# All two-operand element-wise work moved from GpSimd to VectorE in a two-layer decoder step

## The chip, the core and the metric

The kernel runs on one core of a Trainium2 chip. The core has engines with an instruction queue each, worked off in order: TensorE (PE; PEld for its weight loads), VectorE (DVE), ScalarE (ACT), GpSimd (POOL) and SyncE (SP), which here only issues loads and stores. The metric is the device time of one execution in microseconds (us): less is better.

## What is computed

One inference step of a small decoder trunk for 512 prompt tokens and 8 sample tokens, model width 1024, all in float32. Layer A has multi-scale retention beside an attention into 256 memory tokens, layer B an attention to a window of 128 tokens with a sink per head, again beside memory attention. Each is followed by an MLP. Cut to what matters here:

```python
def rmsnorm(x, g):
    y = xf * lax.rsqrt(jnp.mean(xf * xf, axis=-1, keepdims=True) + EPS)
    return y * g

def sq_relu_mlp(x, g, w_up, w_down):          # w_up 1024 x 4096, w_down 4096 x 1024
    h = rmsnorm(x, g) @ w_up
    return jnp.square(jax.nn.relu(h)) @ w_down

def sink_softmax(s, sink):
    m = jnp.maximum(jnp.max(s, axis=-1, keepdims=True), sink)
    e = jnp.exp(s - m)
    return e / (jnp.sum(e, axis=-1, keepdims=True) + jnp.exp(sink - m))

# layer A: o = concat(silu(gate) * groupnorm(retention(q, k, v)), memory_attention)
# layer B: o = concat(window attention with ALiBi and sink_softmax, memory_attention)
# each:    x = x + o @ w_out;  x = x + sq_relu_mlp(x, ...);  at the end: rmsnorm(x, g_final)
```

## The kernel before

Activations lie feature by feature: eight tiles `x[kt]` of 128 partitions x 520 columns (512 prompt and 8 sample tokens), worked on in two halves of 256 and 264 columns. A product keeps nearly float32 precision by splitting each operand into a high part and a rest (both in the type fp32r) and summing three matmuls: high x high, high x rest, rest x high. So each operand, weight or activation, costs one copy on ACT (the high part) and one subtraction of two SBUF operands (the rest): L216 and L217 in `chunk` for weights, L179 and L180 in `Pair.put` for activations.

There are four stages: layer A (0 to about 283 us), the first MLP (265 to 650), layer B (620 to 850) and the second MLP (838 to the end at 1236). An MLP begins in `operands`, where VectorE scales the eight tiles (L278), makes the seven sums and differences of activations (L266) that a product by seven multiplications needs, splits them (L255) and adds up squares for the norm (L384). The first four up-projections of an MLP are direct products (L235), and their results wait for the chain of 1/sqrt (L397 to L365) and for L821. The others go in pairs through `seven`, 28 calls in all: L317 takes the rest of a weight combination, L322 (`total`) makes four sums or differences of weight blocks, 128x512, and L344 to L349 add up the products. Then come L829 (squared ReLU), L830 and the split (L179, L180). The down-projections (`d`) run beside the up-projections of the next group; L438 adds their results out of PSUM onto `x`.

In layer B the weights of the k/v and q projections (`kv0` to `kv3`, `qb0` to `qb7`) are first multiplied with the norm's gains (L214). `win_pair` does window attention for six heads and 128 queries at a time: scores `ws` (L503), copies with the bias out of PSUM (L690), maximum (L694), six exponentials on ACT (L700), the sums' reciprocal (L703), six multiplications by it (L705), transposes on TensorE (L713), copies of these on ACT (L715), products `wo`, and the split into `obh` and `obl`. The out-projection `ob` follows.

A framework of tiles sets the order: it schedules all instructions with a simulated timeline and writes them into the engines' queues. Strings such as ORDER_B only give the order in which the stages' pieces are handed to it. A changed engine or duration can thus change the order in other queues. Which engine does an element-wise step was chosen by tables: `engine()` reads a string with `p` for GpSimd and `v` for VectorE.

```python
ENG_R = dict(a='ppppvppv', m='pppppppv', f='vvvvvvvv', b='vvvvvpvv', y='vppppppv')   # L384
ENG_W = "pvppppvp"                                # L322: three of four on GpSimd
(nc.gpsimd if j % 3 in POOL_N else nc.vector)     # L705, POOL_N = (0, 1): four of six on GpSimd
```

## Time and profile before

| | |
|---|---|
| median of 3 runs | 1240.17 us (1239.22 to 1240.53) |
| the profiled execution | 1238.24 us, its span 1236.4 us |
| TensorE busy | 1196.2 us, 97% of the span |
| VectorE busy | 833.4 us, 67% |
| ACT busy | 534.6 us, 43% |
| GpSimd busy | 229.4 us, 19% |
| mean granted TensorE clock | 0.985 of full speed |

The busy shares are averages over stages with different limits; where TensorE stands idle, and for whom it waits, is read from the timeline of a stage. A timeline row gives the start and the time of an instruction (or of several alike, with their count behind the x), engine, line, operation, what it writes and reads, and in brackets how long the engine was idle before it and what ended that.

### The profile page before, as it was taken

What the parts mean: (1) busy time and instruction counts of PE and PEld (TensorE: products, weight loads), DVE (VectorE), ACT (ScalarE), POOL (GpSimd) and SP (SyncE); (2) the same over time, 40 slices, a digit from 0 to 9 for tenths busy, and PEclk for the clock granted to TensorE, in tenths of its full rate; (3) what the DMA queues carried; (4) which work ended last, traced back from release to release, by engine and by line L of the source; (5) the groups of instructions that cost most, each with busy time, mean ns of one, the idle gap of its engine ahead of it and who ended that gap; (6) DMA issues with size and microseconds to landing.
All of it is one profiled execution on the core that took longest, in us unless ns stands there. A gap on an engine that the chain in (4) does not pass through costs nothing. (4 is left out here: it accounts for less than half of the span.)

```text
span 1236.4 us, 23686 instructions
## 1 busy us (share of the span) xinstructions
PE 1196.2 (97%) x9718; PEld 1138.7 (92%) x9718; DVE 833.4 (67%) x1615; ACT 534.6 (43%) x999; POOL 229.4 (19%) x207
## 2 busy tenths in 40 slices
PE   8999999999999999999999998899799999999996
PEld 7999989999999999999999785579699999999996
DVE  7676777789766666675557558559796566666633
ACT  6232442355554444444324325455464444444532
POOL 2301100001312112121024114110222121121112
PEclk9999999999999999999999999899899999999998
DMA  8344622221223232232324354001132222323402
GB/s 304 112 151 168 217 77 72 88 86 71 73 97 120 86 116 91 97 106 75 121 99 143 107 163 141 30 1 68 36 103 103 82 107 86 120 86 104 140 32 69
DMA packets 43788, 128.25 MB, mean 104 GB/s; under 512 B 5112, under 2 KB 10368, under 8 KB 43552
## 3 DMA queue, kind: packets, MB, share of 16 engines
q1 hardware_dynamic: 41440, 119.80, 27.8%
q0 software_dynamic: 2240, 6.95, 1.5%
q8 instruction: 76, 1.25, 0.4%
q14 instruction: 32, 0.26, 0.1%
HBM read 117.65 MB, written 9.08 MB: 102 GB/s over the span
## 5 line engine op out<-in xcount | busy, mean ns | idle before, releaser
L438 DVE TENSOR_TENSOR xs<-d,xs 128x264 f32<-128x264 f32 (+1 forms) x128 | 54.0, 423 | 102.0 <-PE d L235 102.0
L235 PE MATMUL d<-hid,dw 128*128 128x256 f32 (+1 forms) x384 | 46.9, 283 | 0.0
L235 PEld LDWEIGHTS d<-hid,dw 128*128 128x128 f32 x384 | 46.3, 188 | 0.1
L830 ACT ACTIVATE u<-u 128x520 f32<-128x520 f32 x56 | 35.6, 636 | 21.5 <-DVE u L829 21.5
L639 POOL DMA_DIRECT2D out_ret_s<-s x12 | 6.9, 571 | 135.5 <-DVE s L638 102.8
L235 PE MATMUL ob<-obh,obw 128*128 128x256 f32 (+1 forms) x128 | 26.9, 297 | 2.4 <-ACT obh L179 1.6
L700 ACT ACTIVATE wp<-wp,wnm 128x256 f32<-128x256 f32 (+1 forms) x48 | 22.5, 469 | 12.6 <-DVE wes L697 8.6
L235 PEld LDWEIGHTS ob<-obh,obw 128*128 128x128 f32 x128 | 21.0, 193 | 5.0 <-ACT obh L179 3.0
L705 POOL TENSOR_SCALAR wp<-wp,wsm 128x256 f32<-128x256 f32 (+1 forms) x32 | 15.4, 498 | 54.8 <-ACT wp L700 28.5
L180 DVE TENSOR_TENSOR hid<-u,hid 128x520 fp32r<-128x520 f32 x32 | 23.3, 727 | 0.0
L829 DVE SCALAR_TENSOR_TENSOR u<-u,f0r 128x520 f32<-128x520 f32 x28 | 22.7, 811 | 0.4
L829 DVE SCALAR_TENSOR_TENSOR u<-u,f1r 128x520 f32<-128x520 f32 x28 | 22.7, 811 | 0.4
L524 ACT ACTIVATE p<-ms,nm 128x256 f32<-128x256 f32 x32 | 14.9, 476 | 18.5 <-DVE nm L522 16.8
L713 PEld LDWEIGHTS wt<-c,wp 128*128 128x128 f32 x84 | 9.8, 148 | 12.0 <-POOL wp L705 6.2
L179 ACT CAST hid<-u 128x520 fp32r<-128x520 f32 x32 | 20.1, 628 | 1.0
L713 PE MATMUL wt<-c,wp 128*128 128x128 f32 x84 | 15.7, 300 | 4.7 <-POOL wp L705 2.7
L235 PE MATMUL ob<-obl,obw 128*128 128x256 f32 (+1 forms) x64 | 18.1, 296 | 1.0 <-DVE obl L180 1.0
L522 DVE TENSOR_REDUCE nm<-ms 128x2 f32<-128x512 f32 x16 | 10.3, 685 | 11.8 <-PE ms L503 11.8
L180 DVE TENSOR_TENSOR obl<-wo,obh 128x128 fp32r<-128x128 f32 x24 | 6.9, 287 | 16.2 <-ACT obh L179 16.2
L503 PE MATMUL ws<-kvb,qb 64*128 64x256 f32 (+1 forms) x96 | 15.6, 407 | 1.2 <-DVE wp L690 0.6
L715 ACT COPY wpT<-wt 128x384 f32<-128x384 f32 x28 | 12.8, 479 | 8.2 <-PE wt L713 7.8
L690 DVE SCALAR_TENSOR_TENSOR wp<-cb,ws 128x256 f32<-128x256 f32 (+1 forms) x48 | 15.4, 375 | 0.1
(1997 smaller groups left out, 5124.6 us busy)
## 6 DMA issues: line engine op xcount, KB each, us to landing
kc<-in_mem_k SPq DMA_DIRECT2D x16, 256.0 KB, 4.1
vc<-in_mem_v SPq DMA_DIRECT2D x16, 256.0 KB, 4.4
s<-in_S SPq DMA_DIRECT2D x12, 256.0 KB, 4.9
out_ret_s<-s POOLq DMA_DIRECT2D x12, 256.0 KB, 2.5
xs<-in_xT SPq DMA_DIRECT2D x8, 260.0 KB, 4.3
memx<-in_memT SPq DMA_DIRECT2D x1, 1024.0 KB, 7.6
u004r<-in_w_up SPq DMA_DIRECT2D x2, 512.0 KB, 3.3
u006r<-in_w_up SPq DMA_DIRECT2D x2, 512.0 KB, 3.1
```

Of the source, the lines that this page charges most:

```text
L179: nc.scalar.copy(out=self.hi(kt, sl, rows), in_=src)
L180: eng.tensor_sub(out=self.lo(kt, sl, rows), in0=src, in1=f(self.hi(kt, sl, rows)))
L235: nc.tensor.matmul(t, w[:, ws], a(kt, HALVES[s]), start=kt == k[0] and m == 0, stop=kt == k[-1] and m == 2)
L438: nc.vector.tensor_add(out=x[mb][:, ts], in0=t, in1=x[mb][:, ts])
L503: i = m()
L524: nc.scalar.activation(out=t[:, b, :], in_=s[hh][:, b, :], func=AF.Exp, bias=nm[:, b:b + 1], accum_out=sm[:, b:b + 1])
L690: nc.vector.scalar_tensor_tensor(out=pv[:, j, :], in0=cb["nd"][:, k0:], scalar=float(SLOPES[6 * kb + j]), in1=sv[j // 3][j % 3], op0=ALU.m ...
L700: nc.scalar.activation(out=pv[:, j, :], in_=pv[:, j, :], func=AF.Exp, bias=nm[:, j:j + 1], accum_out=sm[:, j:j + 1])
L705: (nc.gpsimd if j % 3 in POOL_N else nc.vector).tensor_scalar(out=pv[:, j, :], in0=pv[:, j, :], scalar1=sm[:, j:j + 1], scalar2=1.0, op0=A ...
L713: nc.tensor.transpose(t[:, i * P:i * P + P], p[:, 3 * hh + i, kk * P:kk * P + P], ident)
L829: nc.vector.scalar_tensor_tensor(out=u[i], in0=u[i], scalar=0.0, in1=r[0], op0=ALU.max, op1=ALU.mult)
L830: nc.scalar.square(out=u[i], in_=u[i])
```

## The change

VectorE gets what GpSimd did on two operands: three of the four L322 in each call of `seven` (84 instructions), the additions of squares L384 (5 of `aacc`, 6 of `memacc`, 1 of `bacc`, 6 of `y0acc`), the six multiplications L606 in retention, the twelve L214, three L217 (`ob2`, `ob4`, `ob6`), one L180 in layer B and the last multiplications L1023 (8 of the first half, 3 of the second). Of the six multiplications L705 by the softmax's reciprocal, four now run on VectorE and two (j = 2 and 5) on ACT; before it was four on GpSimd and two on VectorE. GpSimd keeps the clearing of tiles and the issue of stores. The tables and `engine()` go, so that a line's number in the new file is about 10 lower (L322 is L312 there, L180 L170, L705 L698 and, for ACT, L696).

```diff
-ENG_R = dict(a='ppppvppv', m='pppppppv', f='vvvvvvvv', b='vvvvvpvv', y='vppppppv')
-ENG_W = "pvppppvp"
-POOL_W = (1, 4, 5)
-POOL_N = (0, 1)
+ACT_N = (2, 5)
...
-                    nc.gpsimd.tensor_tensor(out=w, in0=w, in1=gains[:, GAINS.index(by), :].unsqueeze(2).to_broadcast([P, KT, n // KT]),
+                    nc.vector.tensor_tensor(out=w, in0=w, in1=gains[:, GAINS.index(by), :].unsqueeze(2).to_broadcast([P, KT, n // KT]),
                                             op=ALU.mult)
                 nc.scalar.copy(out=wh[:, s], in_=raw[:, s])
-                eng.tensor_sub(out=wl[:, s], in0=raw[:, s], in1=f(wh[:, s]))
+                nc.vector.tensor_sub(out=wl[:, s], in0=raw[:, s], in1=f(wh[:, s]))
...
             def total(i, x0, x1, alu):
-                engine(ENG_W, i, turn).tensor_tensor(out=s[i], in0=x0, in1=x1, op=alu)
+                nc.vector.tensor_tensor(out=s[i], in0=x0, in1=x1, op=alu)
...
-                    engine(ENG_R[self.name[0]], 0 if self.direct else kt).tensor_add(out=acc, in0=acc, in1=sq)
+                    nc.vector.tensor_add(out=acc, in0=acc, in1=sq)
...
-            nc.gpsimd.tensor_mul(out=qw, in0=q[:, P:T].rearrange("p (n q) -> p n q", q=P),
+            nc.vector.tensor_mul(out=qw, in0=q[:, P:T].rearrange("p (n q) -> p n q", q=P),
...
-                    (nc.gpsimd if j % 3 in POOL_N else nc.vector).tensor_scalar(
-                        out=pv[:, j, :], in0=pv[:, j, :], scalar1=sm[:, j:j + 1], scalar2=1.0, op0=ALU.mult, op1=ALU.mult)
+                    if j in ACT_N:
+                        nc.scalar.mul(out=pv[:, j, :], in_=pv[:, j, :], mul=sm[:, j:j + 1])
+                    else:
+                        nc.vector.tensor_scalar(out=pv[:, j, :], in0=pv[:, j, :], scalar1=sm[:, j:j + 1], scalar2=None, op0=ALU.mult)
...
-                (nc.vector if s and kt not in TAIL_P else nc.gpsimd).tensor_mul(out=y, in0=y, in1=r)
+                nc.vector.tensor_mul(out=y, in0=y, in1=r)
```

VectorE at the start of the second MLP, where the last tiles of `operands` are split and the first call of `seven` (its sums are `u104s`) begins; before:

```order
L255 TENSOR_TENSOR f_10147<-f1t_10183,f_10147 128x260
L266 TENSOR_TENSOR f1t_10213<-f1t_10209,f1xg_10189 128x260
L255 TENSOR_TENSOR f_10122<-f1t_10198,f_10122 128x260
L255 TENSOR_TENSOR f_10134<-f1t_10209,f_10134 128x260
L322 TENSOR_TENSOR u104s_10556<-u104s_10556,u104r_10549 128x512
L180 TENSOR_TENSOR hid_10110<-f1xg_10238,hid_10110 128x520
L255 TENSOR_TENSOR f_10142<-f1xg_10238,f_10142 128x260
```

The same place after:

```order
L312 TENSOR_TENSOR u104s_10556<-u104r_10550 128x512
L374 TENSOR_TENSOR f1acc<-f1acc,f1sq_10229 128x520
L312 TENSOR_TENSOR u104s_10557<-u104r_10549,u104r_10550 128x512
L245 TENSOR_TENSOR f_10147<-f1t_10183,f_10147 128x260
L256 TENSOR_TENSOR f1t_10213<-f1t_10209,f1xg_10189 128x260
L245 TENSOR_TENSOR f_10122<-f1t_10198,f_10122 128x260
L245 TENSOR_TENSOR f_10134<-f1t_10209,f_10134 128x260
L170 TENSOR_TENSOR hid_10110<-f1xg_10238,hid_10110 128x520
L245 TENSOR_TENSOR f_10142<-f1xg_10238,f_10142 128x260
L245 TENSOR_TENSOR f_10150<-f1xg_10238,f_10150 128x260
L312 TENSOR_TENSOR u104s_10556<-u104s_10556,u104r_10549 128x512
```

Two sums of weights now stand ahead of the split L180 of the last tile (L170 after), and the one that stood there before follows it.

ACT in the first block of window attention, where `wp_9080` and `wp_9141` are the score tiles of two groups of six heads and queries, `wpT` the copies of transposes; before:

```order
L700 ACTIVATE wp_9080,wsm<-wp_9080,wnm 128x256 x4
L698 ACTIVATE wes<-wes 128x6
L700 ACTIVATE wp_9141,wsm<-wp_9141,wnm 128x256 x6
L715 COPY wpT_9114<-wt_9110 128x384
L715 COPY wpT_9120<-wt_9116 128x384
L753 ACTIVATE wses<-wsnm,sinks 128x1
L754 ACTIVATE wsp_9338,wssm<-wsp_9338,wsnm 128x129
L715 COPY wpT_9175<-wt_9171 128x384
```

After:

```order
L690 ACTIVATE wp_9080,wsm<-wp_9080,wnm 128x256 x2
L696 ACTIVATE wp_9039<-wp_9039,wsm 128x128 x2
L690 ACTIVATE wp_9080,wsm<-wp_9080,wnm 128x256 x2
L688 ACTIVATE wes<-wes 128x6
L169 CAST obh_8827<-wo_8894 128x128
L690 ACTIVATE wp_9141,wsm<-wp_9141,wnm 128x256
L707 COPY wpT_9114<-wt_9110 128x384
L690 ACTIVATE wp_9141,wsm<-wp_9141,wnm 128x256 x2
L707 COPY wpT_9120<-wt_9116 128x384
L690 ACTIVATE wp_9141,wsm<-wp_9141,wnm 128x256 x3
L696 ACTIVATE wp_9080<-wp_9080,wsm 128x256 x2
L169 CAST obh_8827<-wo_9028 128x128
```

The two multiplications of `wp_9080` (L696) stand behind the last exponential of `wp_9141`; the two of `wp_9141` and then the copy `wpT_9175` follow.

TensorE in the second block, where `wt_9627` and `wt_9633` are the transposes of the softmax tile `wp_9597`; before:

```order
L503 MATMUL ws_9763<-kvb,qb_7822 128x256
L503 MATMUL ws_9761<-kvb,qb_7822 128x256
L713 MATMUL wt_9627<-c,wp_9597 128x128 x3
L235 MATMUL ob_9840<-obh_8155,ob3h 128x256
L235 MATMUL ob_9840<-obl_8157,ob3h 128x256
```

After:

```order
L493 MATMUL ws_9763<-kvb,qb_7822 128x256
L493 MATMUL ws_9761<-kvb,qb_7822 128x256
L225 MATMUL ob_9840<-obh_8155,ob3h 128x256
L225 MATMUL ob_9840<-obl_8157,ob3h 128x256
L225 MATMUL ob_9840<-obh_8155,ob3l 128x256
```

Before the transposes, 14 matmuls of the out-projection `ob` are now in the queue (three of them shown), which stood behind them.

## Rows read from the trace of the kernel before

**Rows 1.** The page's first part: busy us (share) and instructions of each engine.
```profile
PE 1196.2 (97%) x9718; PEld 1138.7 (92%) x9718; DVE 833.4 (67%) x1615; ACT 534.6 (43%) x999; POOL 229.4 (19%) x207
```

**Rows 2.** Table by stretch: us, busy of PE, PEld, DVE, ACT, POOL; PEclk, DMA, GB/s.
```profile
310.00:341.00 31.00, 29.42 (x245) 29.01 (x243) 24.24 (x32) 16.65 (x29) 10.49 (x6) 1.00 0.22 74
...
740.00:770.00 30.00, 25.39 (x191) 17.80 (x189) 25.69 (x57) 16.12 (x44) 11.70 (x10) 1.00 0.38 125
770.00:800.00 30.00, 24.50 (x156) 16.49 (x156) 15.94 (x73) 15.77 (x61) 6.22 (x14) 0.93 0.16 53
800.00:830.00 30.00, 26.92 (x167) 21.00 (x164) 18.75 (x62) 16.03 (x60) 5.82 (x12) 0.84 0.00 1
860.00:890.00 30.00, 21.65 (x141) 20.10 (x140) 25.72 (x61) 12.10 (x26) 7.48 (x3) 0.83 0.18 64
...
1060.00:1160.00 100.00, 100.00 (x834) 99.91 (x833) 64.49 (x82) 44.33 (x67) 18.81 (x14) 1.00 0.26 91
```

**Rows 3.** Timeline of POOL and DVE in the second MLP, two calls of `seven`.
```profile
1080.83 1.29 POOL L322 TENSOR_TENSOR u130s<-u130r 128x512 f32<-128x512 f32 x1 [19.05 <-DMA u130r<-in_w_up]
1082.08 1.30 POOL L322 TENSOR_TENSOR u130s<-u130r,u130r 128x512 f32<-128x512 f32 x1
...
1082.16 1.77 DVE L322 TENSOR_TENSOR u130s<-u130s,u130r 128x512 f32<-128x512 f32 x1 [2.20 <-POOL u130s L322]
...
1106.80 0.68 DVE L322 TENSOR_TENSOR u132s<-u132r,u132s 128x512 f32<-128x512 f32 x1
1107.40 0.42 DVE L438 TENSOR_TENSOR xs<-d,xs 128x264 f32<-128x264 f32 x1
```

**Rows 4.** Timeline of DVE and PE at the start of the first MLP.
```profile
303.09 1.75 DVE L322 TENSOR_TENSOR u004s<-u004s,u004r 128x512 f32<-128x512 f32 x1 [1.18 <-POOL u004s L322]
...
305.29 1.06 DVE L401 SCALAR_TENSOR_TENSOR rv<-rz,rv 104x5 f32<-104x5 f32 x1
...
312.33 0.50 PE L235 MATMUL u<-hid,u002h 128*128 128x256 f32 x2 [0.98 <-DVE u L821]
```

**Rows 5.** Timeline of POOL, DVE and PE at the start of the second MLP.
```profile
866.68 4.59 POOL L322 TENSOR_TENSOR u104s<-u104r 128x512 f32<-128x512 f32 x1 [40.66 <-ACT f L254]
...
871.30 1.74 DVE L322 TENSOR_TENSOR u104s<-u104s,u104r 128x512 f32<-128x512 f32 x1 [1.16 <-POOL u104s L322]
...
873.58 1.85 DVE L255 TENSOR_TENSOR f<-f1xg,f 128x260 fp32r<-128x260 f32 x2
...
873.71 0.38 PE L235 MATMUL u<-hid,u100h 128*128 128x256 f32 x1 [4.10 <-DVE hid L180]
...
915.11 0.39 PE L300 MATMUL u110a<-f,u110l 128*128 128x260 f32 x1 [0.88 <-DVE u110l L317]
```

**Rows 6.** Timeline in window attention; last row, PE's waits: us, times, longest.
```profile
757.36 1.78 DVE L217 TENSOR_TENSOR obw<-ob1r,obw 128x1024 fp32r<-128x1024 f32 x1
759.67 1.21 DVE L217 TENSOR_TENSOR obw<-ob5r,obw 128x1024 fp32r<-128x1024 f32 x1
765.50 1.90 DVE L740 COPY kwc<-kvb 128x2 f32<-128x2 f32 x2
...
773.19 0.49 ACT L700 ACTIVATE wp<-wp,wnm 128x256 f32<-128x256 f32 x1
...
777.33 0.52 PE L713 MATMUL wt<-c,wp 128*128 128x128 f32 x3 [0.89 <-ACT wpT L715]
...
811.51 1.93 POOL L705 TENSOR_SCALAR wp<-wp,wsm 128x256 f32<-128x256 f32 x4 [25.87 <-ACT wp L700]
...
811.35 0.84 DVE L705 TENSOR_SCALAR wp<-wp,wsm 128x256 f32<-128x256 f32 x2
...
815.15 0.33 PE L713 MATMUL wt<-c,wp 128*128 128x128 f32 x1 [1.88 <-POOL wp L705]
...
PE wt L713 <- POOL wp L705: 2.7, 5, 1.9
```

**Rows 7.** Timeline of DVE at the end: the last multiplications.
```profile
1228.81 3.44 DVE L1023 TENSOR_TENSOR xs<-xs,y1r 128x264 f32<-128x264 f32 x5 [1.22 <-ACT y1r L411]
```

More of the change, by code (lines that the diff above doesn't have):

```diff
@@ L46 @@
 ORDER_F = "uddudduddudd"
-ENG_UL = "vvvvvvvv"
-ENG_R = dict(a='ppppvppv', m='pppppppv', f='vvvvvvvv', b='vvvvvpvv', y='vppppppv')
-ENG_B = "pvvvvvvv"
-ENG_W = "pvppppvp"
 BUFS_W = dict(wr=3, wh=3, wl=3)
@@ L56 @@
 BUFS_B = dict(blk=2, wp=3, mp=4, wpT=6, ld=5)
-TAIL_P = (3, 5, 7)
 STORES = ((1, 3, 5, 7), (0, 2, 4, 7))
 KEEP = 4
-POOL_W = (1, 4, 5)
-POOL_N = (0, 1)
+ACT_N = (2, 5)
 ORDER_B = "kasakkskasqqsaqwqwqwwqWwWWwWooSSSoSowWWowoWWoo"
@@ L148, in ld @@
             return blk(name, shape, "ld")
-        def engine(choice, i, turn=0):
-            return nc.gpsimd if choice[len(choice) // 2 * (turn % 2) + i] == "p" else nc.vector
         def small(name, shape, tag=None):
@@ L176, in lo, with put @@
                 return self._at("l", kt)[rows, sl]
-            def put(self, kt, src, sl=slice(0, TT), rows=slice(0, P), eng=nc.vector):
+            def put(self, kt, src, sl=slice(0, TT), rows=slice(0, P)):
                 nc.scalar.copy(out=self.hi(kt, sl, rows), in_=src)
-                eng.tensor_sub(out=self.lo(kt, sl, rows), in0=src, in1=f(self.hi(kt, sl, rows)))
+                nc.vector.tensor_sub(out=self.lo(kt, sl, rows), in0=src, in1=f(self.hi(kt, sl, rows)))
         gains = cp.tile([P, len(GAINS), KT], F32, name="gains")
@@ L202, in gain, with chunk @@
             return gains[:, GAINS.index(name), kt:kt + 1]
-        def chunk(src, n, name, place=None, eng=nc.vector, by=None):
+        def chunk(src, n, name, place=None, by=None):
             raw = wp.tile([P, n], F32, name=f"{name}r", tag="wr", bufs=BUFS_W["wr"])
@@ L249, in split, with cut @@
                 out=a.lo(kt), in0=x[kt], scalar=gain(g, kt), in1=f(a.hi(kt)), op0=ALU.mult, op1=ALU.subtract)
-        def cut(op, j, src, eng):
+        def cut(op, j, src):
             h, l = op[:, 0, j, :], op[:, 1, j, :]
             nc.scalar.copy(out=h, in_=src)
-            eng.tensor_sub(out=l, in0=src, in1=f(h))
+            nc.vector.tensor_sub(out=l, in0=src, in1=f(h))
         def operands(name, g, scale, direct, norm):
@@ L272, in put @@
                     op[i] = half(f"{name}{i}", F32R, [P, 2, UK, EVEN])
-                cut(op[i], j, src, nc.vector)
+                cut(op[i], j, src)
             for n, kt in enumerate(BY_PAIR):
@@ L301, in times, with seven @@
                                      stop=j == nj - 1 and m == 2, skip_group_check=more)
-        def seven(src, op, u, name, turn):
+        def seven(src, op, u, name):
             n = UK * P
@@ L316, in parts @@
                 nc.scalar.copy(out=h[:, c], in_=t)
-                engine(ENG_UL, (1, 5, 3, 4).index(ids[0]), turn).tensor_sub(out=l[:, c], in0=t, in1=f(h[:, c]))
+                nc.vector.tensor_sub(out=l[:, c], in0=t, in1=f(h[:, c]))
                 for i, k in enumerate(ids):
@@ L826, in up @@
                     u = [blk(f"u{l}{g}{n}{i}", tag="u") for i in range(2)]
-                    seven([d["w_up"][l, g * FK + n + i] for i in range(2)], op, u, f"u{l}{g}{n}", n // 2)
+                    seven([d["w_up"][l, g * FK + n + i] for i in range(2)], op, u, f"u{l}{g}{n}")
                     for i in range(2):
@@ L953, in layer_b @@
             for kt in range(KT):
-                b.put(kt, x[kt], eng=engine(ENG_B, kt))
+                b.put(kt, x[kt])
             m = rms("b", "wp")
@@ L1003, in project_out @@
                     t = half(f"obw{n}", F32R, [P, 2, KT * P]) if n < KEEP else None
-                    ahead.append(weights(*src(mb), t if t is None else [t[:, 0], t[:, 1]], nc.gpsimd if n in POOL_W else nc.vector))
+                    ahead.append(weights(*src(mb), t if t is None else [t[:, 0], t[:, 1]]))
                 t = part(f"ob{mb}", s)
```

## The prediction

> **What bounds the kernel now.** I read four views, in this order. The page's first part says who is busy: TensorE 1196.2 of 1236.4 us, VectorE two thirds, GpSimd a fifth [rows 1]. So at most 40.2 us can be had, and only where TensorE stands idle. The table by stretch says where that is [rows 2]. In the steady stretch of the MLP (1060 to 1160) TensorE is busy for all 100 us while VectorE has 35 us free; what is won or lost on VectorE there moves nothing. TensorE is idle for 1.58 us at the start of the first MLP, 4.61, 5.50 and 3.08 in window attention, 8.35 at the start of the second MLP: 23.1 of the 40.2 in five short stretches. In two of them, 740 to 770 and 860 to 890, VectorE is busy for 25.7 us of 30. There VectorE sets the time, and an instruction more or less on it shows.
>
> Third, the timeline of VectorE beside that of GpSimd. In the MLP VectorE's L322, 128x512 with two operands in SBUF, takes 0.68 us at 1106.80, where GpSimd is idle, and 1.77 at 1082.16, where GpSimd began a L322 of its own at 1082.08 [rows 3]. So the engines get in each other's way there, at some 1.1 us a time. GpSimd suffers too: its first `u104s` takes 4.59 us beside a VectorE that is never idle [rows 5], against 1.29 at 1080.83, beside one that waits. Fourth, TensorE's waits, in the stretches named: they end on VectorE, or on GpSimd's softmax operation L705 [rows 4 to 6].
>
> **What VectorE gets, and whether it can carry it.** 84 of L322 at 0.68 [rows 3] are 57.1 us; 12 of L214 and 3 of L217 at 1.21 [rows 6] 18.2; six 128x520 additions of L384 and one L180 at the same price 4.8; 23 operations of 128x256 or 264 (12 of L384, 11 of L1023) at 0.42, the price of an L438 [rows 3], 9.7; six of L606 (128x384) at about 0.55, an estimate between the two sizes, 3.3; 16 more of L705 at 0.42, half of 0.84 [rows 6], 6.7. In all 100 us, so 833 become at most 933, 75% of the span, less what the stretching gives back. ACT gets 16 of L705 at about 0.49, the price of the nearest row, L700 [rows 6]: 8 us. Over the whole, nobody becomes the bound; what counts are the five stretches.
>
> **The steady MLP: nothing.** Per call of `seven` VectorE gets three L322 and loses one or two stretches of 1.1; the next instruction starts 0.60 us after an L322 [rows 3], so that is 1.8 against 1.1 to 2.2. It has a third of its time free, and TensorE is full. Without that cover some 24 steady calls at up to 0.7 us would cost 17 us; the 35 us of free time in 100 speak against it. A wait is added: the first L322 of a call now stands in VectorE's own queue until its weights have landed, with L829 and the L438 that empty TensorE's banks behind it. GpSimd stood so at 1080.83; but VectorE was idle then anyway and waited on, for GpSimd, to 1082.16 [rows 3]. I take 0. Layer B's L214 lies between 638 and 740, where TensorE has matmuls of the last down-projections and of other weights to do; there too I take 0.
>
> **Start of the first MLP: -2.0 us.** VectorE waits 1.18 us for GpSimd's L322 at 303.09, and its own takes 1.75 instead of 0.68 [rows 4]: 2.25 lost. In exchange it gets three L322 at 0.6, 1.8. That looks even, but the chain of 1/sqrt behind it has an instruction on 104x5 elements (L401) of 1.06 [rows 4], stretched like the others, an estimated 0.9. The chain ends 2.25 + 0.9 - 1.8 = 1.3 sooner, and TensorE's wait of 0.98 on L821 behind it goes. A wait for VectorE's L317 like the one of 0.88 at 915.11 [rows 5] stands at 341 too and, following GpSimd's L322, goes as well: 1.0. Bounds: 0, if the three L322 push as much as the stretches return, and -2.2.
>
> **Start of the second MLP: -2.5 us.** The same place, with VectorE full from 838 to 884. There 1.16 (wait) + 1.06 (L322, 1.74) + 1.0 (two L255 of 128x260 in 1.85, against two of 0.42) are lost [rows 5]. The new order puts two L322 ahead of the L180 for which TensorE waits 4.10 us at 873.71, in place of one with its wait (VectorE's queue, before and after, under The change). That L180 comes 1.16 + 1.06 + 0.6 - 2 x 0.6 = 1.6 sooner. At the end of VectorE's chain, where L821 begins, the sum is 3.2 - 3 x 0.6 = 1.4 sooner. To this comes TensorE's wait of 0.88 for `u110l` at 915.11 [rows 5]. Bounds: +1.8 (nothing returns, three L322 more) and -3.2 - 0.9 = -4.1. I take -1.6 - 0.9 = -2.5, since the stretches stand in these very rows.
>
> Here a rule speaks against the change. The Trainium skill, Perfetto Trace Analysis, section Optimizing Scalar/DVE Operations, says that where VectorE is saturated, giving work to ScalarE or even GpSimd may make sense, and adds that between VectorE and GpSimd it might not help since they share a read port. By its first half this place would get 1.8 us slower, by its second half and the rows it gets faster: the trace sides with the second half (1.74 us beside GpSimd against 0.68 alone).
>
> **Window attention, first block (750 to 787): +1.7 us.** Three L217 (ob2, ob4, ob6) enter VectorE's full stretch: 3 x 1.2 = 3.6. It gets back 0.57 of one L217 (1.78 against 1.21 [rows 6]) and about 2 us in tiny operations beside GpSimd (two copies of 128x2 take 1.90 [rows 6]); +1.0 is left. On ACT the order does harm: the two multiplications of a block stand behind the six exponentials of the *next* one (ACT's queue there). GpSimd normalised beside ACT; now the transposes wait for an ACT that is already without a gap (L700 at 0.49, row upon row [rows 6]) and for whose copies TensorE already waits 0.89 at 777.33. Four multiplications of 0.4 and two of 0.33 are an estimated 2.3 us (less than L700, which also sums). Some of it is covered, since VectorE does its four in 1.2 us where GpSimd took 1.93. Bounds: 0 and +4; I take +1.7.
>
> **Window attention, second block (806 to 836): -2.2 us.** TensorE waits 1.88 us at 815.15 for GpSimd, whose four L705 take 1.93 beside VectorE's two in 0.84 [rows 6]. The new order pulls 14 matmuls of `ob` ahead of these transposes (TensorE's queue there), of which 834 run in the 100 us of the steady stretch [rows 2], 0.12 each: 1.7 us of work in this gap, and ACT is free then. All five waits of this kind make 2.7 us [rows 6]; I take 1.7 and 0.5 of the other 0.8. Bounds: -2.7, and 0 if ACT's multiplications come later than GpSimd's did.
>
> **Start and tail: -0.5 us.** In the first 22 us VectorE gets five L384 at 0.6 and loses their stretching of its own instructions: even, 0. At the end its five L1023 took 3.44 us beside GpSimd's three [rows 7]; eight at 0.36, an estimate from the 0.42 less overlap, are 2.9: -0.5. Bounds: -1.5 and +0.5.
>
> Sum: -2.0 - 2.5 + 1.7 - 2.2 - 0.5 = -5.5. The profiled execution took 1238.24 us, so 1232.7; the median of the runs, 1240.17, stands 1.9 above it, so 1234.6.
>
> **Rivals.**
> *Slower, through ACT and VectorE in window attention.* Mechanism: normalisation on ACT behind the next block's exponentials, and three L217 ahead of VectorE's copies out of PSUM. At its bounds the first block costs +4, the second brings nothing; the `ob` work pulled ahead is then missing later, when the exponentials of the third block run, up to +1.9. With start and tail at 0 and the two MLP starts at -1.0 each, the sum is 4 + 1.9 - 2.0 = +3.9: 1244. It decides as soon as ACT's L705 ends later than TensorE has other matmuls to do. For it: ACT's rows without a gap from 770 to 778. Against it: only 16 of 30 us busy there on the whole [rows 2]. 0.18.
> *No difference.* The MLP starts bring -2.5 together, window attention costs +2: 1239 to 1240. For it: TensorE at 97%, and gains at a start that wait next on ACT's copy before L821. 0.18.
> *More.* TensorE's granted clock is 0.83 and 0.84 on the mean of 860 to 890 and 800 to 830 [rows 2]: full clock with pieces at 1.2 instead of 2.4 GHz, which follow idle times. If the idle times go, so may these pieces: 16% of 30 us, some 5 us in each, of which VectorE's chain hides the greater part. With half of it, -5 more: 1229.6. 0.12.
> *The change doesn't do what it says.* The scheduler also reorders the matmuls; the loss could be at any place. It is contained in the first rival's price. 0.02, at 1244.
> My forecast (1231 to 1237): 0.50.
>
> **Numbers.** A measurement tells 0.2% of this kernel, 2.5 us, from no change. Faster: the forecast and the "more" case, 0.62; the same 0.18; slower 0.20. The range of 8 in 10 reaches from 1228 to 1243: below it a third of "more", above it half and more of the slower ones.
>
> **What would show it.** Right: no two-input instruction of VectorE above 1.3 us at 128x512; `u104s` without a wait ahead of it and TensorE's 4.10 at 873 near 2.5; the 1.88 at 815 gone; the rows of 1.85 and 1.75 near 0.8 and 0.7. Wrong: TensorE waiting for ACT in 774 to 786 by more than 2 us above before (the first rival), or TensorE in the MLP below 99%, which would mean that VectorE's queue holds up its copies out of PSUM while an L322 waits for its weights.

## The result: 0.7% slower

The changed kernel takes 1248.45 us (median of 4 runs, 1247.97 to 1250.27), the kernel before 1239.88 beside it. The ratio is 1.0068, with a 95% interval of 1.0055 to 1.0082: some 8.4 us slower, where 5.5 us faster was predicted and 1243 was the upper end of the range. The profiled execution took 1247.97 us, its span is 1246.2, against 1238.24 and 1236.4 before.

The page's first part for the kernel after, busy time and instructions of each engine, which answers to [rows 1]:

```profile
PE 1200.8 (96%) x9718; PEld 1141.4 (92%) x9718; DVE 849.2 (68%) x1766; ACT 538.9 (43%) x1015; POOL 21.4 (2%) x40
```

Two things are to be seen. VectorE took over 100 us of work by the prediction's estimate, and is busy only 15.8 us longer: the stretching did go, and was larger than I thought. And the span grew by 9.8 us. TensorE stands idle for 5.2 of them (45.4 against 40.2) and is busy for 4.6 more with the same 9718 matmuls. Some 2.6 of the 4.6 are its lower clock (mean granted clock 0.983 against 0.985), at places shown below; the other 2.0, of which 1.1 in layer A, where the order of the matmuls changed, can't be put to single rows.

The table by stretch of the kernel after, in the columns of [rows 2] (us, busy of PE, PEld, DVE, ACT, POOL, then PEclk); the last four rows are stretches of [rows 2], the first three are at places that the prediction did not look at:

```profile
250.00:260.00 10.00, 8.00 (x59) 7.35 (x58) 6.94 (x22) 3.04 (x5) 0.00 (x0) 0.94 0.01 2
259.00:262.00 3.00, 3.00 (x15) 3.00 (x15) 3.00 (x6) 2.02 (x5) 0.00 (x0) 0.50 0.07 12
650.00:690.00 40.00, 35.23 (x272) 33.43 (x271) 28.02 (x55) 14.59 (x30) 1.67 (x3) 0.96 0.37 124
...
740.00:770.00 30.00, 27.71 (x201) 21.90 (x201) 19.87 (x59) 15.85 (x46) 2.96 (x4) 1.00 0.27 83
770.00:800.00 30.00, 22.32 (x138) 14.74 (x137) 19.10 (x61) 20.20 (x70) 2.01 (x3) 0.83 0.48 153
860.00:890.00 30.00, 24.98 (x197) 24.27 (x195) 30.00 (x63) 18.23 (x38) 0.00 (x0) 0.95 0.20 72
1060.00:1160.00 100.00, 100.00 (x836) 100.00 (x835) 68.47 (x100) 44.15 (x66) 0.00 (x0) 1.00 0.29 101
```

Two of these places stood in the trace of before as full ones:

```profile
250.00:260.00 10.00, 9.96 (x84) 9.76 (x83) 6.09 (x12) 4.07 (x7) 0.00 (x0) 1.00 0.14 55
650.00:690.00 40.00, 39.74 (x326) 37.00 (x324) 29.87 (x61) 17.71 (x40) 15.35 (x11) 1.00 0.40 135
```

So TensorE lost 2.0 us in 10 at the end of layer A, and 4.5 us in 40 where layer B's projections begin. Of the stretches that the prediction did look at, 740 to 770 and 860 to 890 are fuller than before (27.71 and 24.98 against 25.39 and 21.65), 770 to 800 is emptier (22.32 against 24.50). Such stretches compare roughly only, since the stages lie up to 14 us later by then. To say what each stage contributed, I compared in the two timelines the start of TensorE's first matmul with the same weight tile, and took the differences from one such mark to the next. The last two columns say how much of a difference is idle time of TensorE, and how much is lower clock (half of the time in which it was busy at a granted clock of 0.5); what is left over is neither.

| place | predicted, us | measured, us | of it idle | of it clock |
|---|---|---|---|---|
| start, to the first `qkv00h` | 0 | -2.6 | -1.6 | -1.7 |
| layer A, to `oa1h` at 260 | not priced | +5.3 | +2.5 | +1.7 |
| start of the first MLP, to `u010l` | -2.0 | +1.5 | +0.1 | +1.7 |
| steady first MLP, to 589 | 0 | -0.2 | 0 | 0 |
| layer B, projections (L214), to `qb3h` | 0 | +6.5 | +4.5 | +1.6 |
| window attention, first block, to `ob2h` | +1.7 | +2.8 | +1.1 | +1.4 |
| window attention, second block, to `ob7h` | -2.2 | +0.7 | +0.9 | -0.4 |
| start of the second MLP, to `u110l` | -2.5 | -2.9 | -1.2 | -1.7 |
| steady second MLP | 0 | -0.2 | 0 | 0 |
| tail, to the end | -0.5 | -1.1 | -1.1 | 0 |

The two positive entries that decide, 5.3 and 6.5, are at places to which the prediction gave nothing. The idle column is what an engine's queue can explain. The clock column is less certain to come again: of each kernel one execution was profiled, and the mean granted clock of the four executions of the kernel after lies between 0.978 and 0.983.

### The profile page after: what moved, and what is told of

Its sections match the earlier page's. It is cut to its first block, busy times and chain, and to the rows that moved or that the text cites. A ratio compares the mean times of both kernels' runs of the same rounds, so it can differ in the third digit from the quotient of the medians.

```text
span 1246.2 us, 23531 instructions
## 1 busy us (share of the span) xinstructions
PE 1200.8 (96%) x9718; PEld 1141.4 (92%) x9718; DVE 849.2 (68%) x1766; ACT 538.9 (43%) x1015; POOL 21.4 (2%) x40
## 4 chain that ended last, share of the span: by engine, by line
PE 55%; issue 34%; DVE 7%; ACT 2%; DMA 1%; SPq 0%; DVEq 0%; POOL 0%; POOLq 0%; ACTq 0%
PE d L225 15%; PE qkv L225 9%; PE qb L225 3%; PE ga L225 3%; PE kv L225 1%; PE ob L225 1%; ACT wp L690 1%; PE ms L493 1%; PE memv L478 1%; PE memk L467 1%; DVE wp L680 1%; DVE f L245 1%; PE u L225 1%; PE mt L526 1%; PE mo L493 1%
## 5 line engine op out<-in xcount | busy, mean ns | idle before, releaser
L428 DVE TENSOR_TENSOR xs<-d,xs 128x264 f32<-128x264 f32 (+1 forms) x128 | 54.0, 424 | 107.1 <-PE d L225 107.1
L170 DVE TENSOR_TENSOR hid<-u,hid 128x520 fp32r<-128x520 f32 x32 | 22.1, 692 | 0.0
L705 PEld LDWEIGHTS wt<-c,wp 128*128 128x128 f32 x84 | 10.4, 154 | 12.4 <-ACT wpT L707 6.2
L705 PE MATMUL wt<-c,wp 128*128 128x128 f32 x84 | 16.7, 318 | 4.8 <-ACT wpT L707 4.2
L821 DVE SCALAR_TENSOR_TENSOR u<-u,f0r 128x520 f32<-128x520 f32 x28 | 19.5, 696 | 0.4
L821 DVE SCALAR_TENSOR_TENSOR u<-u,f1r 128x520 f32<-128x520 f32 x28 | 19.5, 696 | 0.4
L170 DVE TENSOR_TENSOR obl<-wo,obh 128x128 fp32r<-128x128 f32 x24 | 6.9, 287 | 15.5 <-ACT obh L169 15.4
L627 DVE TENSOR_TENSOR kvs<-rb,ks 128x512 f32<-128x512 f32 x12 | 8.2, 686 | 9.6 <-PE rb L625 9.6
L493 PEld LDWEIGHTS ws<-kvb,qb 64*128 64x128 f32 x96 | 9.9, 197 | 5.2 <-DVE wp L680 3.0
```

The source lines that it names most:

```text
L170: nc.vector.tensor_sub(out=self.lo(kt, sl, rows), in0=src, in1=f(self.hi(kt, sl, rows)))
L428: nc.vector.tensor_add(out=x[mb][:, ts], in0=t, in1=x[mb][:, ts])
L493: i = m()
L705: nc.tensor.transpose(t[:, i * P:i * P + P], p[:, 3 * hh + i, kk * P:kk * P + P], ident)
L821: nc.vector.scalar_tensor_tensor(out=u[i], in0=u[i], scalar=0.0, in1=r[0], op0=ALU.max, op1=ALU.mult)
```

## The experiments

### One part at a time

Six kernels are the kernel before with one part of the change. The ratios compare with executions of the kernel before made beside each run (medians 1239.47 to 1240.34), and the microseconds behind a ratio are worked out from it. All twelve L214 on VectorE:

```diff
-                    nc.gpsimd.tensor_tensor(out=w, in0=w, in1=gains[:, GAINS.index(by), :]...
+                    nc.vector.tensor_tensor(out=w, in0=w, in1=gains[:, GAINS.index(by), :]...
```

> The kernel before, with nothing changed but the twelve L214 (weights times gains) moved from GpSimd to VectorE. Theory A: an L214 stands at the head of VectorE's queue until its weights have landed, and what empties TensorE's banks and the 1/sqrt chain wait behind it: +5 to +7 us against the kernel before (about 1245 to 1247), VectorE idle on DMA for some 10 us between 635 and 690, and TensorE behind by 5 to 7 us from the k/v projection on. Theory B: it is only the added work, 12 x 1.2 us on a VectorE with free time: 0 to +2 us, no idle time of VectorE on DMA ahead of the 1/sqrt chain.

Measured: 1242.39 us, ratio 1.0022 (1.0005 to 1.0039), +2.7 us.

The softmax's normalisation as after: four of six on VectorE, two on ACT.

```diff
-                    (nc.gpsimd if j % 3 in POOL_N else nc.vector).tensor_scalar(
...
+                    if j in ACT_N:
+                        nc.scalar.mul(out=pv[:, j, :], in_=pv[:, j, :], mul=sm[:, j:j + 1])
+                    else:
+                        nc.vector.tensor_scalar(out=pv[:, j, :], in0=pv[:, j, :], scalar1=sm[:, j:j + 1], scalar2=None, op0=ALU.mult)
```

> The kernel before, with only the softmax multiplication L705 as in the changed kernel: four of six on VectorE, two on ACT. Theory A: the two on ACT stand behind the next block's exponentials and hold the transposes up: +2 to +4 us (1242 to 1244), with TensorE's waits for ACT's copies of transposes up by 2 us. Theory B: the loss in window attention comes from the three L217 in VectorE's full stretch, and L705 alone gives -2 to 0 us, since GpSimd's 1.93 us go.

Measured: 1242.89 us, ratio 1.0028 (1.0012 to 1.0044), +3.5 us.

The six multiplications L606 of retention on VectorE:

```diff
-            nc.gpsimd.tensor_mul(out=qw, in0=q[:, P:T]...
+            nc.vector.tensor_mul(out=qw, in0=q[:, P:T]...
```

> The kernel before, with only the six L606 of retention moved to VectorE. Theory A: it is L606 that changes the order of TensorE's matmuls in layer A, so that other work runs out before the last head of retention is done: +3 to +5 us (1243 to 1245), TensorE idle for about 2 us between 240 and 262. Theory B: the order changes through the additions of squares L384 at the start; L606 alone gives -0.5 to +0.5 us.

Measured: 1241.90 us, ratio 1.0031 (1.0019 to 1.0044), +3.9 us, for six instructions of half a microsecond. The ten executions reach from 1239.87 to 1245.41, and the difference of the medians is 2.4 only; the profiled one is the slowest of them.

All sums of weights L322 on VectorE:

```diff
-ENG_W = "pvppppvp"
+ENG_W = "vvvvvvvv"
```

> The kernel before, with only L322 (all four sums of a call) on VectorE. Theory A: stretching and waiting at the start of the second MLP go, nothing else changes: -2 to -4 us (1236 to 1238), TensorE's wait for the split L180 at 873 from 4.1 to about 2.5 us, steady MLP at 100%. Theory B: the gain seen there in the changed kernel came with its other order of things, or is lost again at the start of the first MLP: -0.5 to +1 us.

Measured: 1238.30 us, ratio 0.9991 (0.9981 to 1.0001), -1.1 us: no difference that can be told.

The three L217 on VectorE:

```diff
-POOL_W = (1, 4, 5)
+POOL_W = ()
```

> The kernel before, with only the three L217 of ob2, ob4 and ob6 moved to VectorE. Theory A: they stand in VectorE's full stretch of window attention, but their own stretching of other instructions goes: 0 to +1.5 us. Theory B: they hold up the copies out of PSUM by their whole 3.6 us: +2 to +4 us.

Measured: 1241.43 us, ratio 1.0009 (1.0000 to 1.0018), +1.1 us.

Start and tail: the additions of squares L384 (one of them in layer B), layer B's one L180 and the last multiplications L1023:

```diff
-ENG_R = dict(a='ppppvppv', m='pppppppv', f='vvvvvvvv', b='vvvvvpvv', y='vppppppv')
-ENG_B = "pvvvvvvv"
+ENG_R = dict(a='vvvvvvvv', m='vvvvvvvv', f='vvvvvvvv', b='vvvvvvvv', y='vvvvvvvv')
+ENG_B = "vvvvvvvv"
...
-                (nc.vector if s and kt not in TAIL_P else nc.gpsimd).tensor_mul(out=y, in0=y, in1=r)
+                nc.vector.tensor_mul(out=y, in0=y, in1=r)
```

> The kernel before, with the sums of squares L384, the L180 and the last multiplications L1023 on VectorE; L322, L214, L217, L606 and L705 stay where they were. Theory A: the 2.4 us that the changed kernel gained in its first 22 us and the 1.1 us at its end come from these: -2.5 to -4 us (1235.5 to 1237). Theory B: the gain at the start came with the other order in retention (L606): -1 to 0 us.

Measured: 1235.97 us, ratio 0.9967 (0.9956 to 0.9979), -4.1 us.

What follows: the six sum up to +6.0 us, the whole change costs +8.4. The difference of 2.4 lies within the intervals taken together (about 4), so the parts nearly add up. Three parts cost, L214, L606 and the softmax; one gains, the ends; L322, with 84 instructions the largest part by far, makes no difference that can be told. The softmax, L606 and L217 fell into the range of their first theory, the ends just beyond it; L214 and L322 fell between their two theories, so their times decide nothing.

### Layer B: work or waiting?

Why L214 costs is read from VectorE's timeline in the kernel after. The rows that matter from 655 to 676:

```profile
655.26 1.23 DVE L204 TENSOR_TENSOR kv2r<-kv2r,gains 128x1024 f32<-128x1024 f32 x1 [2.77 <-DMA kv2r<-in_w_kv]
...
668.04 0.69 DVE L374 TENSOR_TENSOR bacc<-bacc,bsq 128x520 f32<-128x520 f32 x1
668.75 1.23 DVE L204 TENSOR_TENSOR qb0r<-qb0r,gains 128x1024 f32<-128x1024 f32 x1
671.42 1.23 DVE L204 TENSOR_TENSOR qb1r<-qb1r,gains 128x1024 f32<-128x1024 f32 x1 [1.45 <-DMA qb1r<-in_w_in_b]
...
673.70 0.16 DVE L387 TENSOR_SCALAR rv<-bms 104x5 f32<-104x5 f32 x1
...
675.91 0.17 DVE L355 SCALAR_TENSOR_TENSOR ry<-rqt,rqu 104x5 f32<-104x5 f32 x1
```

The multiplications (L204 now) stand ahead of the norm's chain: the squares `bacc` end at 668.73, the chain of 1/sqrt begins with `rv` at 673.70 and ends with `ry` at 676.08. In between VectorE waits for a weight to land. TensorE at the same place, after:

```profile
673.42 0.28 PE L225 MATMUL kv<-bh,kv1l 128*128 128x256 f32 x1
676.13 0.66 PE L399 MATMUL bmt<-c,ry 104*128 104x104 f32 x5 [2.43 <-DVE ry L355]
678.89 0.59 PE L225 MATMUL kv<-bh,kv1h 128*128 128x264 f32 x1 [2.11 <-DVE kvb L411]
```

And before, VectorE's end of the chain and the matmul that takes it:

```profile
668.03 0.17 DVE L365 SCALAR_TENSOR_TENSOR ry<-rqt,rqu 104x5 f32<-104x5 f32 x1
...
668.25 0.66 PE L409 MATMUL bmt<-c,ry 104*128 104x104 f32 x5
```

Before, `ry` ended at 668.20 and `bmt` began at 668.25: TensorE waited for nothing, but there was nothing to spare either: 0.05 us also stand between `ry` and `bmt` after (676.08 to 676.13), where TensorE does wait for it. After, it waits 2.43 and, one step later, 2.11 us, and then runs at half its clock:

```profile
679.00:682.00 3.00, 3.00 (x14) 3.00 (x15) 2.32 (x8) 0.00 (x0) 0.00 (x0) 0.50 0.00 0
```

In that stretch it does 14 matmuls in 3 us; 32 run in the 4 us that follow. At half clock 3 us lose 1.5, which makes 6.0 with the two waits, of the 6.5 in the table. So the place is found. Is it the work on VectorE, or its waiting for DMAs at the head of its queue? In the next kernel VectorE does twelve multiplications of the same size that need no DMA; their results are not used, so this kernel leaves the gains out of layer B's weights and serves for its time alone:

```diff
-                    w = raw.rearrange("p (k c) -> p k c", k=KT)
-                    nc.gpsimd.tensor_tensor(out=w, in0=w, in1=gains[:, GAINS.index(by), :]...
+                    w = now["w"].tile([P, n], F32, name="free", tag="free", bufs=1).rearrange("p (k c) -> p k c", k=KT)
+                    g = gains[:, GAINS.index(by), :].unsqueeze(2).to_broadcast([P, KT, n // KT])
+                    nc.vector.tensor_tensor(out=w, in0=g, in1=g, op=ALU.mult)
```

> The kernel before without L214 on GpSimd: in its place VectorE does twelve multiplications of the same size, 128x1024, on the gains alone, into a tile that nobody reads; so they wait for no load (the gains are left out of the weights of layer B). Nine of them stand ahead of the 1/sqrt chain of layer B. Theory A (the waiting at the head of the queue costs, not the work): -1 to +2 us against the kernel before, and TensorE at the k/v projection behind by no more than 1.5 us, where the kernel with L214 on VectorE was behind by 4.8. Theory B (the work of 12 x 1.2 us costs): +3 to +8 us.

Measured: 1248.92 us, ratio 1.0067 (1.0054 to 1.0080), +8.3 us. Its timeline, VectorE and then TensorE:

```profile
670.36 0.15 DVE L397 TENSOR_SCALAR rv<-bms 104x5 f32<-104x5 f32 x1
670.47 1.23 DVE L215 TENSOR_TENSOR free<-gains 128x1024 f32<-128x1024 f32 x1
671.62 0.17 DVE L357 TENSOR_SCALAR rqj<-rv 104x5 int32<-104x5 int32 x1
671.74 1.23 DVE L215 TENSOR_TENSOR free<-gains 128x1024 f32<-128x1024 f32 x1
...
675.95 1.13 PE L409 MATMUL bmt<-c,ry 104*128 104x104 f32 x5 [6.85 <-DVE ry L365]
```

All twelve of them stand ahead of the chain's end, three even between its steps, and TensorE waits 6.85 us. The theory that only waiting costs fell: work alone, in this place, is enough. Two more kernels then divide L214 by place, not by kind; only the chunks named differ:

```diff
-                    nc.gpsimd.tensor_tensor(out=w, ...
+                    (nc.gpsimd if name in ('qb2', 'qb3', 'qb4', 'qb5') else nc.vector).tensor_tensor(out=w, ...
```

> The kernel before, with the other eight L214 on VectorE: qb6, qb7, kv0 to kv3, qb0 and qb1, which stand ahead of the end of the 1/sqrt chain. Theory A: the whole cost of the kernel with all twelve, +2.5 to +5 us, TensorE 3 to 5 us behind at kv3 with a wait for the chain's end (L409) of a us or more. Theory B: two thirds of it, +1.8 to +3 us.

Measured: 1244.15 us, ratio 1.0036 (1.0021 to 1.0050), +4.5 us. And the other way round, `qb2` to `qb5` on VectorE and the rest on GpSimd:

> The kernel before, with four of the twelve L214 on VectorE: those of qb2 to qb5, which stand behind the 1/sqrt chain of layer B in VectorE's queue. Theory A (only what stands ahead of the chain's end costs, since TensorE waits for that chain without any slack): -0.7 to +0.7 us, and TensorE at kv3 not behind. Theory B (each L214 on VectorE costs its share): a third of the kernel with all twelve, +1 to +1.5 us.

Measured: 1240.18 us, ratio 0.9997 (0.9987 to 1.0008), -0.4 us. TensorE's wait for the chain in the two traces, ahead and then behind:

```profile
671.37 0.66 PE L409 MATMUL bmt<-c,ry 104*128 104x104 f32 x5 [1.10 <-DVE ry L365]
...
669.01 0.66 PE L409 MATMUL bmt<-c,ry 104*128 104x104 f32 x5 [0.25 <-DVE ry L365]
```

What follows: the L214 that stand ahead of the chain's end cost all that this part costs, the four behind it cost nothing that can be told. By the times alone an equal share of each of the twelve (0.9 us for four of them) is not ruled out, since the interval for the four ends at +1.0. The traces tell the two apart: between `u010l` and `qb3h` TensorE is idle for 2.8 us with the eight ahead, for 1.1 with the four behind and for 0.3 before. The trace with the eight is that of the fastest of nine executions (1241.09). A part of its loss may be a changed order: 641 of the 9718 matmuls stand at another place in TensorE's queue there, 37 with the four.

### Layer A: the instruction or the order?

In the kernel after, and in the one with L606 alone, the scheduler puts the products of the last head later in TensorE's queue. Before, 1929 matmuls stand ahead of the last `ro` (L646) and 2025 ahead of the first of the out-projection, `oa0h`; with L606 moved it is 2027 and 1999, so that the last head comes behind. Two kernels move only some heads. With heads 0, 2, 3 and 5 the last head stays ahead of `oa0h` (1926 and 2025), with heads 1, 2 and 4 it comes late (2026 and 1999). The last head's own multiplication is on VectorE in the first of the two and on GpSimd in the second. The rest of layer A's queue is not left as it was by either: of its first 2200 matmuls 1340 keep their place in the first, 805 in the second and 786 in the kernel after.

```diff
-            nc.gpsimd.tensor_mul(out=qw, in0=q[:, P:T]...
+            (nc.vector if h in (0,2,3,5,) else nc.gpsimd).tensor_mul(out=qw, in0=q[:, P:T]...
```

> The kernel before, with L606 on VectorE for four of the six heads (0, 2, 3, 5). With these four the scheduler leaves the last head's products in TensorE's queue where they were, some 95 rows ahead of the out-projection `oa`. Theory A (the order costs, not the operation): -0.7 to +0.7 us against the kernel before, no wait for `oah` near 258. Theory B (the operation on VectorE costs): two thirds of what all six cost (+3.9), +2 to +3 us.

Measured: 1240.48 us, ratio 1.0010 (0.9998 to 1.0021), +1.2 us. With `h in (1,2,4,)` in the same place:

> The kernel before, with L606 on VectorE for three heads only (1, 2, 4). With these three the scheduler puts the last head's products behind the first 15 rows of the out-projection, as with all six. Theory A (the order costs): +3 to +5 us, though half of the operations stay on GpSimd, and TensorE waiting some 2 us for `oah` near 258. Theory B (the operation costs): half of what all six cost, +1.5 to +2.5 us, and no such wait.

Measured: 1247.34 us, ratio 1.0065 (1.0050 to 1.0080), +8.1 us. Fewer instructions moved, and a loss several times as large. Both times lie outside the ranges expected: the first between the two theories, the second above both. TensorE's timeline in the late order, where the last head's results are transposed (L667) and the out-projection takes them:

```profile
259.25 0.60 PE L667 MATMUL rx<-c,on 128*128 128x128 f32 x4
259.68 0.38 PE L667 MATMUL ry<-c,op 128*128 128x128 f32 x2
261.91 0.51 PE L235 MATMUL oa<-oah,oa0h 128*128 128x256 f32 x2 [1.85 <-ACT oah L179]
...
264.12 0.42 PE L235 MATMUL oa<-oah,oa4l 128*128 128x264 f32 x1
264.34 0.42 PE L235 MATMUL oa<-oah,oa4h 128*128 128x264 f32 x1
```

TensorE waits 1.85 us for ACT's copy of the last head, since nothing else is left to do, and then starts a matmul every 0.22 us. In the kernel after the same row stands at 256.69, with the same 1.85, and the granted clock from 259 to 262 is 0.50 (the table above). In the order kept TensorE waits for nothing there. From the 2001st matmul to the 2141st, around this wait, the three kernels with the late place fall 4.2 (heads 1, 2 and 4), 3.8 (all six heads) and 4.2 us (the kernel after) further behind the kernel before; the one that keeps the place, with the last head's multiplication on VectorE, falls behind by 0.0. So at this place the order costs, not the multiplication. Ahead of it, from `qkv00h` on, the same traces lose 3.9, 1.0 and 1.1 us, and the one that keeps the place 2.8. The order of matmuls differs there too, and whether that order or the multiplication is to blame was not separated.

### Window attention: ACT, or any engine but GpSimd?

If ACT's queue alone were the cost, normalising on VectorE alone should cost nothing:

```diff
-POOL_N = (0, 1)
+POOL_N = ()
```

> The kernel before, with all six softmax multiplications L705 on VectorE and none on ACT or GpSimd. Theory A (what costs in the changed kernel is that two of them stand in ACT's queue behind the next block's exponentials): -1.5 to +1 us against the kernel before, where the kernel with four on VectorE and two on ACT was 3.5 us slower. Theory B (VectorE's added operations cost, wherever the rest runs): +3 to +5 us.

Measured: 1242.18 us, ratio 1.0022 (1.0010 to 1.0034), +2.7 us, beside +3.5 with ACT, and between the two theories. TensorE waits for VectorE now; VectorE's row and TensorE's, and in the last row the wait at the same place with the softmax as after, on VectorE and ACT:

```profile
754.80 3.55 DVE L705 TENSOR_SCALAR wp<-wp,wsm 128x256 f32<-128x256 f32 x6
757.09 2.03 PE L713 MATMUL wt<-c,wp 128*128 128x128 f32 x9 [2.39 <-DVE wp L705]
...
756.89 3.06 PE L715 MATMUL wt<-c,wp 128*128 128x128 f32 x12 [2.39 <-DVE wp L708]
```

So in these two kernels it is not ACT alone. But both keep an L217 of GpSimd beside VectorE's multiplications (from 753.56 to 756.88 where all six are on VectorE), and it stretches them. In the kernel after L217 runs on VectorE, the same multiplications take 1.13 us (four), and TensorE waits 0.50 there. So a part of what these kernels lose the kernel after does not have, and what of the +3.5 is ACT's part stays open. Against this stands the second block of the kernel after, where ACT is at fault visibly. ACT's timeline, and then TensorE's:

```profile
833.98 0.51 ACT L690 ACTIVATE wp<-wp,wnm 128x256 f32<-128x256 f32 x1 [3.46 <-DVE wes L687]
...
836.55 0.49 ACT L690 ACTIVATE wp<-wp,wnm 128x256 f32<-128x256 f32 x1
...
837.04 0.83 ACT L707 COPY wpT<-wt 128x384 f32<-128x384 f32 x2
...
837.55 0.55 PE L705 MATMUL wt<-c,wp 128*128 128x128 f32 x3 [2.26 <-ACT wpT L707]
```

The copies `wpT` stand behind six exponentials, from 833.98 to 837.04 without a gap, and TensorE waits 2.26 us for them.

### The parts that gain, put together

The last kernel takes the start, the tail and all L322, and leaves L214, L606, L217 and the softmax on GpSimd; its diff is that of the kernel with start and tail and the line of `ENG_W`.

> As the run before this one, and with L322 on VectorE too; L214, L217, L606 and L705 stay on GpSimd. If the parts add up, -3 from the ends and -1 to -3 from L322 at the start of the second MLP: -4 to -6 us (1233.5 to 1235.5). If the gains don't add (the start of the MLP is bound by something else): no better than the run with the ends alone.

Measured: 1234.97 us, ratio 0.9955 (0.9941 to 0.9969), -5.6 us. It beats both kernels. The two parts alone add up to -5.2, so the gains add.

## Why the prediction was wrong

**"TensorE is full, so it is hidden" (layer B's L214): this step failed, by 6.5 us.** The sentence was that TensorE "has matmuls of the last down-projections and of other weights to do". It had; but the chain behind which the next work stands ended 0.05 us before TensorE needed it. An engine without idle time shows only that what it waits for comes in time, not by how much. The rows at 668 were in the trace, and I priced the step without looking for the first thing that TensorE takes from VectorE there. The stretching went as predicted even here: the chain from `rv` to `ry` takes 2.38 us after and took 5.15 before (663.05 to 668.20). It began 10.65 us later, of which 4.0 is how far the whole kernel was behind at 589.

**Layer A was not priced at all: +5.3.** The six L606 had an entry in VectorE's load, and none among the places. The rival that the scheduler's new order would cost something somewhere got 0.02 and a price borrowed from another rival. It alone was worth some 4 us at one place in each of the three kernels with the late order, and the order of TensorE's queue could have been read before the run. The idle time of 2.5 and the 1.7 us lost at half clock explain 4.2 of the 5.3; the rest, 1.1, lies ahead of that place, and I did not find it in single rows.

**Start of the first MLP: -2.0 became +1.5.** VectorE's timeline after, around the chain:

```profile
307.48 0.17 DVE L387 TENSOR_SCALAR rv<-f0ms 104x5 f32<-104x5 f32 x1 [1.06 <-PE f0ms L384]
308.35 1.22 DVE L207 TENSOR_TENSOR u003l<-u003r,u003h 128x1024 fp32r<-128x1024 f32 x1 [0.70 <-ACT u003h L206]
309.49 0.68 DVE L312 TENSOR_TENSOR u004s<-u004r,u004s 128x512 f32<-128x512 f32 x1
```

The stretches of [rows 4] are gone: L312 takes 0.68 instead of 1.75, and the 1.06 of L401 is 0.16 now. But the chain now begins with a wait of 1.06 for TensorE's sum of squares, and one of the sums got in between its steps. TensorE, just behind:

```profile
314.37 0.66 PE L399 MATMUL f0mt<-c,ry 104*128 104x104 f32 x5 [1.22 <-DVE ry L355]
316.01 0.50 PE L225 MATMUL u<-hid,u002h 128*128 128x256 f32 x2 [0.98 <-DVE u L813]
```

The wait of 0.98 was to go and stayed to the hundredth, as it hangs on ACT's copy `f0r` and the step behind it, not on when the chain ends. The wait for `u010l` at 341, 0.91 before, did go; the 1.22 is new. So the idle time is the same, 2.2 us against 2.1, and what this place lost is the clock behind the two waits, 0.50 from 316.9 to 320.3. With L322 alone on VectorE (`sums_only`) it was the same: 2.2 us idle, half clock from 313.9 to 317.3, and a loss of 1.4. But it is not a fixed price of the sums. The kernel with the parts that gain has all of them on VectorE and the same two waits:

```profile
309.33 0.66 PE L409 MATMUL f0mt<-c,ry 104*128 104x104 f32 x5 [1.22 <-DVE ry L365]
310.97 0.50 PE L235 MATMUL u<-hid,u002h 128*128 128x256 f32 x2 [0.97 <-DVE u L821]
```

There the granted clock stayed at 1.00, and this place cost nothing (-0.1).

**Window attention: the first block right in direction, the second wrong.** The price of 0.42 us for an L705 was read from a row beside GpSimd; alone it takes 0.28 (four in 1.13). First block +2.8 against +1.7, within the bounds given; 1.1 of it is idle time and 1.4 lower clock, for which the forecast had no term. TensorE's longest wait there ends on a chain of VectorE's:

```profile
775.62 1.22 DVE L207 TENSOR_TENSOR ob2l<-ob2r,ob2h 128x1024 fp32r<-128x1024 f32 x1
...
777.08 1.22 DVE L207 TENSOR_TENSOR ob6l<-ob6r,ob6h 128x1024 fp32r<-128x1024 f32 x1
...
782.93 0.29 DVE L170 TENSOR_TENSOR obl<-wo,obh 128x128 fp32r<-128x128 f32 x1
...
783.27 1.08 PE L736 MATMUL wss<-kwc,qdw 128*32 128x129 f32 x8 [3.17 <-DVE obl L170]
```

Two of the three L217 that moved stand ahead of the step for which TensorE waits 3.17 us, as the prediction said of this block. That they cause the wait is not shown: alone they cost 1.1 us in all. In the second block the 1.88 of [rows 6] did go, since the `ob` matmuls were pulled ahead. But the first of them waits 1.00 us itself (at 826.84, for VectorE's L428), and they were then missing later: the 2.26 at 837.55 shown above stands there. This is the first rival's clause ("the `ob` work pulled ahead is then missing later, when the exponentials of the third block run, up to +1.9"); the forecast took the gain of the reordering and left its cost to the rival. TensorE's waits for ACT's `wpT` make 4.2 us after and made 2.0 before, so the mark set for that rival, 2 us above before, was reached, though mostly later than the stretch named for it.

**Start of the second MLP: the number right, by luck in part.** It gained 2.9 where 2.5 was predicted:

```profile
881.80 0.39 PE L225 MATMUL u<-hid,u100h 128*128 128x256 f32 x1 [2.00 <-DVE hid L170]
882.00 0.68 DVE L312 TENSOR_TENSOR u104s<-u104r 128x512 f32<-128x512 f32 x1
885.79 0.76 DVE L245 TENSOR_TENSOR f<-f1xg,f 128x260 fp32r<-128x260 f32 x2
885.92 0.39 PE L225 MATMUL u<-hid,u100h 128*128 128x256 f32 x1 [2.41 <-DVE hid L170]
```

The 4.10 of [rows 5] is 2.41 (near 2.5 was said), L312 has no wait ahead of it, the pair of 1.85 takes 0.76, and the 0.88 for `u110l` went; the 2.00 at 881.80 stood there before too. These are the 2.5 us that were priced. But other waits grew in their place: TensorE's for the end of the chain from 0.53 to 1.52 us, and a new one of 0.55 for `u103l`. So the idle time fell by 1.2 only. The other 1.7 are clock: 10.2 us at half clock before, 6.8 after. The kernel with L322 alone and the one with the parts that gain have the same fall in idle time here, but not the better clock, and gained 1.3 and 1.4. One reading of [rows 5] was wrong: beside the 4.59 us of `u104s` VectorE was not always busy, but idle for the last 1.16 of them. At this place the half of the rule cited from the Trainium skill that speaks for shared reads held in direction, as the forecast took it.

**Right: the steady MLP and the tail.** In the steady MLP TensorE is busy for all 100 us. The tail's last multiplications, of [rows 7]:

```profile
1239.71 2.84 DVE L1015 TENSOR_TENSOR xs<-xs,y1r 128x264 f32<-128x264 f32 x8 [1.22 <-ACT y1r L401]
```

Eight in 2.84 us against the 2.9 worked out. The start, which I put at 0, gained 2.6: TensorE's wait of 2.0 us for ACT's `ah` fell to 1.0, those for `al`, 0.7 together, went, and half clock from 7.5 to 10.9 us stands in the trace before and not in the one after. With that, start and tail gained 3.7 where the bound was 1.5.

In short: the mechanism was right (GpSimd beside VectorE stretches VectorE), and most of the waits that it was to remove did go or shrink. But at the starts of the MLPs and in the second block others took the place of a part or all of them: the sum counted every wait removed as time won. The first MLP's start and the second block lie outside their stated bounds by 1.5 and 0.7 us on the one side, start and tail by 2.2 on the other. The sum failed on two places that had been written off because TensorE showed no idle time there, 11.8 us together.

## What to carry to other kernels

A full engine is no proof of slack: before moving work to an engine that feeds it, compare the end of the producer's chain with the start of its consumer, and where the distance is zero, price what is put ahead of the chain (here eight instructions of 1.23 us cost 4.5). An instruction put on another engine also moves others in a scheduled kernel, so read the new order of the bounding engine at the end of each stage, where the last result is awaited and nothing else is left. Move by place: moves of the same kind won 4.1 us with the sums and multiplications at the ends of this kernel and lost 4.5 ahead of one chain. A wait removed is won only if no other takes its place, so add up TensorE's idle time of the whole stage, and read its clock apart from it.

## What the runs showed of the hardware

The price of two engines at work together was larger than I had thought. The 151 instructions that VectorE took over last 99 us in the kernel after, near the 100 estimated; as busy time, in which the overlap of one with the next counts once, they are 89. Its busy time rose by 15.8, so some 73 us of its 833 had been stretching beside GpSimd. The Trainium skill, SBUF — State Buffer, section Who interferes with whom, says that a VectorE instruction with two inputs in SBUF contends with a GpSimd instruction that reads SBUF; the traces agree (1.75 against 0.68 for L322) and give the price.

A multiplication with a single tile as input is stretched too: six L705 of 128x256 took 3.55 us on VectorE while GpSimd still ran L217, against this row of the same trace, at which GpSimd rests:

```profile
776.80 1.67 DVE L705 TENSOR_SCALAR wp<-wp,wsm 128x256 f32<-128x256 f32 x6
```

The same section of the Trainium skill says that such operations can enter a mode with both ports, in which whichever engine issues first blocks the other fully; 0.59 against 0.28 each agrees with contention, and no run here tells in which mode it ran.

An idle time of some 2 us can cost TensorE nearly as much again: after waits of 2.43 and 2.11 us the granted clock was 0.50 from 679 to 682, after one of 1.85 it was 0.50 from 259 to 262, that is the lower of its two levels, 1.2 instead of 2.4 GHz, and 1.5 us of each 3 us were lost. It need not: the same two waits, 1.22 and 0.98 us, were followed by half clock in two traces (the kernel after and the one with L322 alone) and by full clock in a third (the kernel with the parts that gain).
